# Six edits in one step: a whole-bank gather, S5 powers taken in a pair ahead, one table for small inputs, forget terms in two float32r parts, the last ada chunks inside the routing

## The chip, the cores and the metric

One core of one Trainium2 chip runs the whole program in one launch. The metric is device time in microseconds (us), the median over runs. Everything is float32 in HBM; 580 MB of weights are streamed once through the core's on-chip memory in chunks of [128, 4096] float32 (2 MiB), and the tokens (256 of them, 1024 wide) stay on chip.

## The reference, cut to what matters

Two networks in a row over x [1, 256, 1024]. The first has two blocks, each with a mixer (attention, then pooling) and a mixture of 32 experts, and takes shift, scale and gate from an "ada" product of the condition vector c:

```python
def first_block(x, c, ...):
    c_act = jax.nn.silu(c)
    for i in range(2):
        mod = c_act @ ada_w[i] + ada_b[i]                 # ada_w[i]: [1024, 6*1024]
        sh_m, sc_m, gt_m, sh_f, sc_f, gt_f = jnp.split(mod, 6, axis=-1)
        h = modulate(rmsnorm(x, norm_mix_g[i]), sh_m, sc_m)
        y = fox_attention(h, ...) if i == 0 else pool_mixer(h, ...)
        x = x + gt_m[:, None, :] * y
        h = modulate(rmsnorm(x, norm_ffn_g[i]), sh_f, sc_f)
        y = grouped_moe(h, router_w, router_bias, exp_w1[i], exp_w3[i], exp_w2[i])
        x = x + gt_f[:, None, :] * y
    return rmsnorm(x, norm_final_g)

def fox_attention(h, w_in, f_bias, w_o):                  # 16 heads of 64
    q, k, v, f = jnp.split(h @ w_in, [D, 2 * D, 3 * D], axis=-1)
    F = jnp.cumsum(jax.nn.log_sigmoid(f + f_bias), axis=1)
    logits = q @ k.T * scale + F[t] - F[s]                # the forget terms, causal
    return softmax(logits) @ v @ w_o

def grouped_moe(h, router_w, router_bias, w1, w3, w2):    # best group of 8, then top 2 of 32
    scores = jax.nn.sigmoid(h @ router_w)
    # choose by scores + router_bias; gate = scores of the chosen two, normed
    return sum over the chosen e of gate[e] * ((silu(h @ w1[e]) * (h @ w3[e])) @ w2[e])
```

The second network adds an mLSTM beside an S5 state-space mixer, a feed-forward block, an HGRN2 mixer and another feed-forward block. Of it only the set-up of the S5 coefficients is touched here: the powers of its diagonal and the tap matrices K, which depend on weights alone and are made during the first network's second expert layer.

## The kernel before, in words

**Stages.** Attention with the ada product of both layers (20 to 221 us), routing of layer 0 (to 259), experts of layer 0 (to 698), pooling (to 721), routing of layer 1 (to 766), experts of layer 1 (to about 1247), then the second network (to 1935).

**The weight stream.** Chunks are declared in a fixed order (`need`) and issued as soon as a slot is free (`prefetch`, L204, on SP's DMA queue); `get` hands out a chunk, `free` gives its slot back. There are seven slots (`ringa` 3, `ringb` 4) from the start, and three more (`ringc`) from the end of attention to expert pair 3 of layer 1. SP takes its DMA instructions in order, so a chunk whose slot is not free holds up those behind it. In attention the order is the first four ada chunks, attention weights with ada chunks 4 to 15 between them, the first half of the output weights, ada 16 to 21, the second half of them, ada 22 and 23; then the experts' chunks, six for each pair of experts, 16 pairs a layer.

**Order of the work.** In `attention` and `experts` PE's order is written out by hand (`manual_schedule`). The rest is ordered by a scheduler that simulates the program and takes what it holds to be ready; `tc.issue_after(mark)` keeps an instruction behind a given one. The other engines wait on semaphores.

**Attention.** `att_start` loads x, makes the squares for the norm on DVE (L370) and ACT (L368), and takes ada chunks 0 to 3 on PE (`ada_mm`, L655: the activated c, spread to 32 columns as `crep`, against a chunk; a copy on ACT; then a `turn`, L673, of eight small matmuls that brings the row into columns). Ada chunks 4 to 17 are taken on DVE against `crow`, the row of c spread over all partitions; 18 to 23 on PE again, in three pairs near the end of attention. `forget_gate` makes F, `forget_rows` (L849) spreads F by selection matrices `fsel` into two rows per head, `LA` and `RA`, and `heads` adds the forget terms to the logits with one more matmul of two rows (L869). ACT's DMA queue carries, in this order, the table of vectors `vec`, and small inputs: bif, rw, rb, crow, attn_f, fbias, fsel.

**Routing.** `route` makes the router's products (L948) and the transposed tokens, picks the experts on DVE with many small operations, and counts the tokens per expert (L1006). Beside it `moe` splits the transposed tokens into a high and a low float32r part: two copies on ACT (`full`, `hth`), a subtraction on POOL (L1036, `htl`). `overflow` loads the largest count into a register of every engine and branches on it (L1202, L1203); the branch is not taken here.

**Experts.** Two pairs at a time: `gather` (L1086) multiplies the tokens by a one-hot matrix, for four PSUM banks `pd` of two halves each, four matmuls per half. The eviction of a half is written behind its four matmuls:

```python
for b in range(4):
    pd = pp.tile([128, 2, 256], F32, name="e1", bufs=2)
    for i in range(2):
        ... four matmuls into pd[:, i, :]
        if i: nc.scalar.activation(hg..., pd[:, i, :], ...)      # L1089
        else: nc.vector.tensor_scalar(hg..., pd[:, i, :], ...)   # L1091
```

Then for each pair `up` (L1119, four chunks), `turned` (L1132) and `down` (L1146, two chunks), and `spread_out` (L1170) adds a pair's result. Of the eight gathers of a layer one comes ahead of the loop, and seven in it.

**S5 set-up.** A generator that advances one step per expert pair in layer 1 (pairs 7 to 12). Its tap steps fill one PSUM bank `pk` by pieces (L1449) and add the diagonal on DVE, piece by piece (L1457, `s5K`). Its four power steps each multiply on POOL and DVE (L1383, L1387) into one `stage` and transpose the result on PE (L1474), all in one step.

Of the kernel before, what the change touches and what calls it, by code (L numbers as in the profile page):

```python
# [10 lines left out]
F32 = mybir.dt.float32  # L11
# [33 lines left out]
for _name, _cols in [  # L45
# [3 lines left out]
    ("are", 16), ("aim", 16), ("ldt", 16),  # L49
# [6 lines left out]
def layout(x):  # L56
# [25 lines left out]
    }  # L82
    vec = np.zeros((128, NVEC), np.float32)
# [7 lines left out]
    o["crow"] = g["c"]  # L91
# [3 lines left out]
    sel = np.zeros((17, 2, 4, 128), np.float32)  # L95
    for hd in range(NH):
        q, i = 2 * (hd % 2) + hd // 2 % 2, hd // 4
        sel[hd, 0, i, 32 * q] = 8.0
        sel[16, 0, i, 32 * q + 1] = 1.0
        sel[16, 1, i, 32 * q] = 1.0  # L100
        sel[hd, 1, i, 32 * q + 1] = -8.0
    o["fsel"] = sel
    o["fbias"] = g["attn_f_bias"][0].reshape(NH, 1)
    o["wo"] = kxn(g["attn_w_o"][0], 1024).reshape(128, 2, 4096).transpose(1, 0, 2)
    o["rw"] = g["router_w"].reshape(8, 128, NE).transpose(1, 0, 2)
    o["rb"] = g["router_bias"].reshape(1, NE)
# [32 lines left out]
    bif = np.zeros((36, 1), np.float32)  # L139
    bif[0:4, 0] = g["ab_b_if_2"][0][0:4]  # L140
    bif[32:36, 0] = g["ab_b_if_2"][0][4:8]
    o["bif"] = bif
# [20 lines left out]
class Net:  # L163
# [114 lines left out]
    def consts(self):  # L278
# [345 lines left out]
    def ada_setup(self, P):  # L624
        nc = self.nc
        ca = P.tile([128, KT], F32, name="ca")
        nc.scalar.activation(ca, self.vec("c"), AF.Silu)
        self.crep = P.tile([128, KT, 32], F32, name="crep")
        nc.vector.tensor_copy(self.crep, ca[:, :, None].to_broadcast([128, KT, 32]))
        self.crow = P.tile([128, D], F32, name="crow")  # L630
        nc.scalar.dma_start(self.crow, self.A["crow"].to_broadcast([128, D]))
        nc.scalar.activation(self.crow, self.crow, AF.Silu)
        self.halfsel = P.tile([128, 2], F32, name="halfsel")
# [21 lines left out]
    def ada_mm(self, chunks, wp, pp):  # L655
# [3 lines left out]
        pg = pp.tile([128, 512], F32, name="pL", bufs=2)  # L659
# [7 lines left out]
        row = wp.tile([128, 512], F32, name="adarow", bufs=2)  # L667
        nc.scalar.copy(row, pg)

        def turn():  # L670
            pm = pp.tile([128, n, 4], F32, name="gm")
# [17 lines left out]
    def attention(self):  # L689
        nc, tc = self.nc, self.tc  # L690
        with ExitStack() as es:
# [5 lines left out]
            LA = wp.tile([128, 4, T], F32, name="LA")  # L697
            RA = wp.tile([128, 4, T], F32, name="RA")
# [4 lines left out]
            fb = wp.tile([NH, 1], F32, name="fb")  # L703
            nc.scalar.dma_start(fb, self.A["fbias"])
            fsel = wp.tile([NH + 1, 2, 4, 128], F32, name="fsel")
            nc.scalar.dma_start(fsel, self.A["fsel"])
            with ExitStack() as es1:
                w0 = self.pool(es1, "att0", 1)
                self.maskA = self.mask(wp, self.ramp(w0), OP.is_gt, 8.0 * BIG, nc.gpsimd)
                self.att_start(h, w0, pp)  # L710
# [50 lines left out]
            qk(0, 1, range(4))  # L761
            self.forget_rows(F1, LA, RA, fsel, pp)
# [7 lines left out]
            values(0, 0, range(8))  # L770
            do(1)
            values(0, 1, range(8))
# [1533 lines left out]
```

## Time and profile before

| | us |
|---|---|
| median of three runs | 1944.87 |
| the three runs | 1947.57, 1936.15, 1944.87 |
| profiled execution, its own time | 1936.65 |
| its span in the trace | 1934.9 |
| PE busy in it | 1757.8 (91%) |
| VectorE (DVE) busy | 795.3 (41%) |
| ScalarE (ACT) busy | 541.3 (28%) |
| GpSimd (POOL) busy | 176.5 (9%) |
| mean granted TensorE clock | 0.959 |

The span runs from the first to the last instruction that the profiler shows; the profiled execution's own time has 1.75 us more around it. Busy time of TensorE (PE) is counted apart from its weight loads (PEld), which overlap it. A line such as L1119 is a line of the kernel's code; an arrow `out<-in` names the tiles written and read. In a timeline the brackets hold how long the engine stood idle ahead of the instruction and what released it.

### The profile page before, as it was taken

The page shows a single profiled execution, that of the slowest core. Times are in us where ns is not written, and L with a number is a line of the kernel's source. Part 1 is how long each engine was busy: PE and PEld are TensorE (multiplying, and loading weights), DVE is VectorE, ACT ScalarE, POOL GpSimd, SP SyncE. Part 2 cuts the span into 40 slices and gives each one's busy share as a digit, 9 for nine tenths or more (in the row PEclk, how much of TensorE's full clock was granted, in tenths as well). Part 3 has the DMA queues.
Part 4 walks back from the last instruction along what each step waited for, and adds up shares of the span by engine and source line. Part 5 has one row for each costly group of instructions (what it writes and reads, how often), then busy time and mean ns, then how long its engine had stood idle before and what let it go on. Part 6 is the DMA issues. An engine that isn't in the chain of part 4 may idle for free.

```text
span 1934.9 us, 26697 instructions
## 1 busy us (share of the span) xinstructions
PE 1757.8 (91%) x11274; PEld 1177.5 (61%) x11274; DVE 795.3 (41%) x1532; ACT 541.3 (28%) x958; POOL 176.5 (9%) x263
## 2 busy tenths in 40 slices
PE   4999689999999985999988889899999989999998
PEld 2676434444444454444444333488999989999997
DVE  3676422112111133222542223366655556665554
ACT  2222211111110122101200001154644456555443
POOL 0000100000000001000240333213100002200000
PEclk9899879999999996999989989998999999999999
DMA  9996969999999994999899879822555434344541
GB/s 394 425 349 255 399 262 426 427 427 426 427 427 427 427 426 164 428 426 428 371 400 385 352 306 427 343 71 88 194 195 195 153 137 174 131 192 154 200 169 44
DMA packets 42130, 582.92 MB, mean 301 GB/s; under 512 B 4865, under 2 KB 5249, under 8 KB 6418
## 3 DMA queue, kind: packets, MB, share of 16 engines
q1 hardware_dynamic: 41184, 580.13, 72.9%
q8 instruction: 92, 1.51, 0.3%
q10 hardware_dynamic: 818, 0.98, 0.1%
q14 instruction: 36, 0.29, 0.0%
HBM read 580.05 MB, written 1.05 MB: 300 GB/s over the span
## 4 chain that ended last, share of the span: by engine, by line
PE 52%; DVE 5%; ACT 2%; issue 2%; POOL 1%; DVEq 0%; ACTq 0%; POOLq 0%
PE e L1119 11%; PE py L1898 6%; PE e L1146 6%; PE ph L263 4%; PE ph L264 4%; PE ph L265 4%; PE e L1086 2%; PE q L264 2%; PE q L265 2%; PE q L263 2%; PE yacc L1165 2%; DVE wlo L241 1%; DVE hg L1091 1%; POOL ringb L1387 1%; DVE ringb L1383 1%
## 5 line engine op out<-in xcount | busy, mean ns | idle before, releaser
L241 DVE TENSOR_TENSOR wlo<-ringa,whi 128x1024 fp32r<-128x1024 f32 x190 | 225.9, 1229 | 177.0 <-ACT whi L240 176.9
L240 ACT CAST whi<-ringa 128x1024 fp32r<-128x1024 f32 x192 | 191.5, 1049 | 143.2 <-issue 60.6
L1119 PE MATMUL e<-ringb,hg 128*64 128x512 f32 x1024 | 227.7, 599 | 2.4 <-issue 1.2
L264 PE MATMUL ph<-hlo,whi 128*128 128x256 f32 x704 | 198.0, 281 | 0.6 <-DVE hlo L546 0.6
L263 PE MATMUL ph<-hhi,whi 128*128 128x256 f32 x704 | 198.3, 282 | 0.0
L265 PE MATMUL ph<-hhi,wlo 128*128 128x256 f32 x704 | 197.9, 281 | 0.0
L1126 DVE TENSOR_TENSOR u<-u,e 128x512 f32<-128x512 f32 x32 | 22.0, 688 | 386.2 <-PE e L1119 386.2
L1119 PEld LDWEIGHTS e<-ringb,hg 128*64 128x64 f32 x1024 | 78.8, 139 | 144.2 <-issue 141.2
L264 PEld LDWEIGHTS ph<-hlo,whi 128*128 128x128 f32 x704 | 133.9, 190 | 1.6 <-DVE hlo L546 0.8
L263 PEld LDWEIGHTS ph<-hhi,whi 128*128 128x128 f32 x704 | 134.1, 190 | 0.8
L265 PEld LDWEIGHTS ph<-hhi,wlo 128*128 128x128 f32 x704 | 134.1, 190 | 0.0
L1119 PE MATMUL e<-ringa,hg 128*64 128x512 f32 x592 | 132.9, 598 | 1.0 <-DMA ringa<-in_exp 1.0
L1086 PE MATMUL e<-oh,hth 128*128 128x256 f32 x256 | 80.2, 339 | 55.3 <-DVE hg L1091 43.2
L1146 PE MATMUL e<-ringa,uT 128*64 128x512 f32 x528 | 117.7, 596 | 3.6 <-issue 3.6
L1086 PEld LDWEIGHTS e<-oh,hth 128*128 128x128 f32 x256 | 53.8, 210 | 80.8 <-DVE hg L1091 57.1
L1119 PEld LDWEIGHTS e<-ringa,hg 128*64 128x64 f32 x592 | 45.2, 138 | 83.6 <-issue 83.2
L1119 PE MATMUL e<-ringc,hg 128*64 128x512 f32 x432 | 95.2, 592 | 0.0
L1089 ACT ACTIVATE hg<-e,mod,msc 128x256 f32<-128x256 f32 x64 | 36.2, 565 | 186.7 <-PE e L1086 186.6
L1123 ACT ACTIVATE u<-e 128x512 f32<-128x512 f32 x32 | 19.1, 597 | 233.4 <-PE e L1119 233.4
L1146 PEld LDWEIGHTS e<-ringa,uT 128*64 128x64 f32 x528 | 39.6, 137 | 70.2 <-issue 68.3
L1156 ACT ACTIVATE yh<-e,gs 128x512 fp32r<-128x512 f32 x32 | 22.0, 687 | 202.0 <-PE e L1146 202.0
L1387 POOL TENSOR_TENSOR ringb<-ringb 128x128 f32<-128x128 f32 (+1 forms) x86 | 46.0, 548 | 343.2 <-DVE ringb L1383 220.5
(572 smaller groups left out, 3267.2 us busy)
## 6 DMA issues: line engine op xcount, KB each, us to landing
ringb<-in_exp SPq DMA_DIRECT2D x83, 2048.0 KB, 17.9
ringa<-in_exp SPq DMA_DIRECT2D x70, 2048.0 KB, 15.6
ringc<-in_exp SPq DMA_DIRECT2D x39, 2048.0 KB, 23.4
ringa<-in_f SPq DMA_DIRECT2D x32, 2048.0 KB, 7.4
ringb<-in_ada SPq DMA_DIRECT2D x15, 2048.0 KB, 11.7
ringa<-in_ada SPq DMA_DIRECT2D x9, 2048.0 KB, 16.3
ringa<-in_cin SPq DMA_DIRECT2D x8, 2048.0 KB, 8.2
ringa<-in_attn SPq DMA_DIRECT2D x3, 2048.0 KB, 15.7
```

What stands on the lines that cost most here:

```text
L240: nc.scalar.copy(hi[:, o], raw[:, o])
L241: (eng or nc.vector).tensor_tensor(lo[:, o], raw[:, o], hi[:, o], op=OP.subtract)
L263: mm(ps, wh, ah, start=start, stop=False, **kw)
L264: mm(ps, wh, al, start=False, stop=False, **kw)
L265: mm(ps, wl, ah, start=False, stop=stop, **kw)
L1086: nc.tensor.matmul(pd[:, i, :], htok[h][:, tt, k * 128:(k + 1) * 128], oh[:, tt, :], start=tt + h == 0, stop=tt + h == 2)
L1089: nc.scalar.activation(hg[q][:, k, :], pd[:, i, :], AF.Identity, scale=sc[:, k:k + 1], bias=sh[:, k:k + 1])
L1119: nc.tensor.matmul(ps[s, :], h[:, kt, o:o + 64], w[:, k, ab, :], start=kt == 0, stop=kt == KT - 1)
L1146: nc.tensor.matmul(py[s, :], uT[:, ft, s], w[:, ft, ab, :], start=ft == 0, stop=ft == 3)
L1165: nc.tensor.matmul(yacc[tt][hf], g[:, 128 * tt:128 * tt + 128], y[p][i][:, 512 * hf:512 * hf + 512], start=False, stop=last and i == 1, sk ...
L1387: nc.gpsimd.tensor_tensor(o, a, b, op=op)
L1898: m = nc.tensor.matmul(py[tt][hf], u[x][:, ts_], w[y][:, n], start=ft == 0 and i == 0, stop=ft == NFT - 1 and i == 2)
```

## The change

Six edits are made together.

- **Table.** bif, fbias, the router's bias and weights become columns of `vec` (336 columns before, 626 after), which SP loads ahead of x. ACT's queue is left with two loads, attn_f and fsel. crow is no longer loaded: `spread_row` makes it from the activated c, with eight matmuls and two copies. `crep` goes; the matmul reads the column of c with a broadcast.
- **Forget terms.** F is split into a high and a low float32r part in 48 rows, the selection matrices are float32r with four rows per head, and `LA` and `RA` are float32r. The first values product moves ahead of `forget_rows`.
- **Ada.** Chunks 18 to 23 leave `attention`; `ada_rest` takes them in the routing of layer 0, behind the last transpose of the tokens.
- **Low part of the tokens.** One DVE operation from PSUM in the place of ACT's second copy and POOL's subtraction: two of them are held behind the gate's last operation, two behind `slot`.
- **Gather.** Both evictions of a bank are written behind all eight matmuls.
- **S5.** Taps: the diagonal is added behind all four pieces. Powers: two rooms in place of one stage; the powers of a step are multiplied one or more pairs ahead of the step that transposes them.

```diff
@@ the table VEC
-    ("are", 16), ("aim", 16), ("ldt", 16),
+    ("are", 16), ("aim", 16), ("ldt", 16), ("bif", 1), ("fb", 1), ("rb", NE), ("rw", KT * NE),
...
-    o["crow"] = g["c"]
...
-        nc.scalar.dma_start(self.vt, self.A["vec"])
-        self.bif = P.tile([36, 1], F32, name="bif")
-        if "bif" in self.A:
-            nc.scalar.dma_start(self.bif, self.A["bif"])
+        nc.sync.dma_start(self.vt, self.A["vec"])
+        self.bif = self.vec("bif")
...
     def ada_setup(self, P):
-        ca = P.tile([128, KT], F32, name="ca")
+        ca = self.P1.tile([128, KT], F32, name="ca")
         nc.scalar.activation(ca, self.vec("c"), AF.Silu)
-        self.crep = P.tile([128, KT, 32], F32, name="crep")
-        nc.vector.tensor_copy(self.crep, ca[:, :, None].to_broadcast([128, KT, 32]))
-        self.crow = P.tile([128, D], F32, name="crow")
-        nc.scalar.dma_start(self.crow, self.A["crow"].to_broadcast([128, D]))
-        nc.scalar.activation(self.crow, self.crow, AF.Silu)
...
+    def ada_rest(self, wp, pp):
+        turn = [self.ada_mm(ADA[i:i + 2], wp, pp, ("a0", 1, "m0")) for i in range(18, 24, 2)]
+        for t in turn:
+            t()
...
-                nc.tensor.matmul(pg[q:q + 32, :], self.crep[:, kt, :], w[:, kt, :], start=kt < 4 // n, stop=kt >= KT - 4 // n)
+                nc.tensor.matmul(pg[q:q + 32, :], self.ca[:, kt:kt + 1].to_broadcast([128, 32]), w[:, kt, :], start=kt < 4 // n, stop=kt >= KT - 4 // n)
...
@@ attention
-            LA = wp.tile([128, 4, T], F32, name="LA")
-            RA = wp.tile([128, 4, T], F32, name="RA")
+            LA = wp.tile([128, 4, T], F32R, name="LA")
+            RA = wp.tile([128, 4, T], F32R, name="RA")
...
-            fb = wp.tile([NH, 1], F32, name="fb")
-            nc.scalar.dma_start(fb, self.A["fbias"])
-            fsel = wp.tile([NH + 1, 2, 4, 128], F32, name="fsel")
-            nc.scalar.dma_start(fsel, self.A["fsel"])
+            fb = self.vec("fb")[0:NH, :]
+            fraw = wp.tile([48, 2, 4, 128], F32, name="fraw")
+            nc.scalar.dma_start(fraw, self.A["fsel"])
+            fsel = wp.tile([48, 2, 4, 128], F32R, name="fsel")
+            nc.scalar.copy(fsel, fraw)
...
             qk(0, 1, range(4))
+            values(0, 0, range(8))
             self.forget_rows(F1, LA, RA, fsel, pp)
...
             do(0)
-            values(0, 0, range(8))
+            values(0, 1, range(8))
             do(1)
-            values(0, 1, range(8))
...
             ada(2)
-            t1 = self.ada_mm(ADA[18:20], wp, pp)
+            wo(1, range(0, 4), range(2))
             do(7)
-            t2 = self.ada_mm(ADA[20:22], wp, pp)
+            wo(1, range(4, 8), range(2))
             do(7)
-            t1()
-            wo(1, range(KT), range(2))
-            t2()
             self.route_setup(0, wp, pp, "gm")
             wo(1, range(KT), range(2, 4))
-            self.ada_mm(ADA[22:24], wp, pp)()
...
@@ att_start
+        self.spread_row(crow, self.ca, pp, "pL", 2)
...
@@ forget_gate
+        F1 = wp.tile([48, T], F32R, name="fF1")
+        nc.scalar.activation(F1, self.ones[0:48, 0:1].to_broadcast([48, T]), AF.Copy)
+        nc.scalar.copy(F1[0:NH, :], C)
+        nc.vector.tensor_tensor(F1[32:32 + NH, :], C, F1[0:NH, :], op=OP.subtract)
...
@@ heads
-                b = slice(b, b + 2)
+                b = slice(b, b + 4)
...
@@ moe_setup
-        self.rw = P.tile([128, KT, NE], F32, name="rw")
-        nc.scalar.dma_start(self.rw, self.A["rw"])
-        self.rbias = P.tile([128, NE], F32, name="rbias")
-        nc.scalar.dma_start(self.rbias, self.A["rb"].to_broadcast([128, NE]))
+        self.rw = self.vec("rw").rearrange("p (k n) -> p k n", k=KT)
+        self.rbias = self.vec("rb")
...
@@ route
+        if meanwhile:
+            with tc.issue_after(t.ins):
+                meanwhile(w2, pp)
...
@@ moe
-                gate, slot, mint, r, mark = self.route(wp, w2, pp, xt)
-                with tc.issue_after(mark):
-                    for i in range(4):
-                        o = slice((i % 2) * 512, (i % 2) * 512 + 512)
-                        src, sc = xt[i].rearrange("p a b -> p (a b)"), r[:, i // 2:i // 2 + 1]
-                        full = w2.tile([128, 512], F32, name="full", bufs=2)
-                        nc.scalar.activation(full, src, AF.Copy, scale=sc)
-                        nc.scalar.activation(htok[0][:, i // 2, o], src, AF.Copy, scale=sc)
-                        nc.gpsimd.tensor_tensor(htok[1][:, i // 2, o], full, htok[0][:, i // 2, o], op=OP.subtract)
+                gate, slot, mint, r, marks = self.route(wp, w2, pp, xt, None if l else self.ada_rest)
+                for i, mark in ((0, 1), (2, 1), (1, 2), (3, 2)):
+                    o = slice((i % 2) * 512, (i % 2) * 512 + 512)
+                    src, sc = xt[i].rearrange("p a b -> p (a b)"), r[:, i // 2:i // 2 + 1]
+                    hi, lo = (htok[h][:, i // 2, o] for h in range(2))
+                    with tc.issue_after(marks[0]):
+                        nc.scalar.activation(hi, src, AF.Copy, scale=sc)
+                    with tc.issue_after(marks[mark]):
+                        nc.vector.scalar_tensor_tensor(lo, src, sc, hi, op0=OP.mult, op1=OP.subtract)
...
@@ gather
+                for i in range(2):
+                    k = 2 * b + i
                     if i:
                         nc.scalar.activation(hg[q][:, k, :], pd[:, i, :], AF.Identity, scale=sc[:, k:k + 1], bias=sh[:, k:k + 1])
...
@@ the S5 set-up
+            for jt in range(js, js + 4):
                 nc.vector.scalar_tensor_tensor(s5["K"][:, jt, :], self.ident, self.vec("dskip", jt, 1), pk[:, jt - js, :],
                                                op0=OP.mult, op1=OP.add)
...
+        rooms = [buf[:, o:o + 1024].rearrange("p (i j n) -> p i j n", i=2, j=4) for o in (1024, 2048)]
+        def powers(q):
...
+                o = [rooms[q % 2][:, i, :, 32 * j:32 * j + 32] for i in range(2)]
...
+        def turned(q):
...
+                    nc.tensor.transpose(pt[:, jt, :], rooms[q % 2][:, i, jt, :], self.ident)
+                nc.vector.tensor_copy(s5["B"][:, i, 4 * q:4 * q + 4, :], pt)
+        taps(0)
+        powers(0)
+        yield True
+        taps(4)
+        yield True
+        taps(8)
+        yield True
+        taps(12)
+        powers(1)
+        yield True
+        for q in range(4):
+            turned(q)
+            if q < 2:
+                powers(q + 2)
             yield True
```

`spread_row` is there before too (it makes the gate's row in layer 1): for each of eight columns a matmul of the column, broadcast, with the identity, and a copy for each half of the row.

## Rows read from the trace of the kernel before

**Rows 1.** Windows of the whole span: us, each engine's busy us, granted clock, DMA share, GB/s.

```profile
core 0: us, PE busy (x) PEld busy (x) DVE busy (x) ACT busy (x) POOL busy (x), PEclk, DMA share, GB/s
0.00:43.00 43.00, 17.44 (x168) 9.18 (x168) 9.54 (x53) 11.05 (x19) 2.74 (x11) 1.00 0.96 391
...
95.00:192.00 97.00, 97.00 (x494) 63.84 (x492) 66.82 (x184) 25.31 (x88) 0.62 (x1) 1.00 0.78 302
...
247.00:264.00 17.00, 13.74 (x50) 8.67 (x52) 5.71 (x14) 4.82 (x6) 0.00 (x0) 0.57 0.02 8
264.00:691.00 427.00, 401.64 (x2072) 183.98 (x2070) 80.66 (x144) 45.99 (x74) 0.00 (x0) 1.00 1.00 425
...
766.00:1247.00 481.00, 437.61 (x2476) 199.29 (x2474) 145.79 (x305) 53.92 (x87) 89.25 (x154) 0.97 0.92 386
```

**Rows 2.** Waits of PE, 264 to 700: waited for, us in total, times, longest us.

```profile
PE e L1086 <- DVE hg L1091: 17.9, 28, 0.7
...
PE e L1119 <- DMA ringb<-in_exp: 1.2, 1, 1.2
```

**Rows 3.** Timeline, 0 to 60: start, us, engine, line, operation, out<-in, count [idle before<-releaser].

```profile
10.24 0.75 DVE L370 TENSOR_TENSOR nsq<-x 128x256 f32<-128x256 f32 x2
...
19.96 0.72 ACT L368 ACTIVATE nsq<-x 128x256 f32<-128x256 f32 x2 [10.96 <-DMA rbias<-in_rb]
...
43.42 15.70 PE L607 MATMUL pL<-h,ringa 128*128 128x256 f32 x64 [0.99 <-DVE h L827]
```

**Rows 4.** Timeline of PE, 59 to 130, the forget terms and the first values.

```profile
80.34 6.71 PE L849 MATMUL pL<-fF,fsel 17*128 17x256 f32 x16 [3.65 <-issue]
...
90.74 8.99 PE L732 MATMUL pL<-ringb,h 128*128 128x512 f32 x16
101.77 7.13 PE L732 MATMUL pL<-ringb,h 128*128 128x512 f32 x16
```

**Rows 5.** Groups of PE, 43 to 222: line, operation, count | busy us, mean ns.

```profile
L869 PE MATMUL pQ<-RA,LA 2*128 2x128 f32 (+1 forms) x64 | 10.4, 402 | 0.0
```

**Rows 6.** Timeline of PE, 168 to 265, from the ada chunks to the experts.

```profile
188.51 3.64 PE L664 MATMUL pL<-ringa,crep 128*32 128x512 f32 x32
...
205.17 0.95 PE L673 MATMUL gm<-halfsel,adarow 128*128 128x2 f32 x8
...
215.39 3.64 PE L664 MATMUL pL<-ringb,crep 128*32 128x512 f32 x32
...
220.80 1.07 PE L948 MATMUL m<-x,rws 128*32 128x256 f32 x16
...
236.60 0.41 PE L1006 MATMUL m<-am,ones 128*1 128x32 f32 x4 [10.38 <-DVE am L997]
...
258.79 3.40 PE L1119 MATMUL e<-ringa,hg 128*64 128x512 f32 x8
```

**Rows 7.** Timeline of DVE, 218 to 265, routing of layer 0 and first gather.

```profile
229.56 2.35 DVE L978 SCALAR_TENSOR_TENSOR gq<-gs,gm,revg 128x4 f32<-128x4 f32 x2
...
234.85 0.29 DVE L989 MAX8 v<-selm 128x8 f32<-128x32 f32 x2
...
244.67 0.76 DVE L1071 TENSOR_TENSOR oh<-iota,slot 128x256 fp32r<-128x256 f32 x2 [5.63 <-PEq L1203]
...
256.47 0.76 DVE L1071 TENSOR_TENSOR oh<-iota,slot 128x256 f32<-128x256 f32 x2 [1.31 <-PE e L1086]
```

**Rows 8.** Timeline of POOL, 218 to 265, the first of two subtractions.

```profile
229.40 2.49 POOL L1036 TENSOR_TENSOR htl<-full,hth 128x512 fp32r<-128x512 f32 x2 [6.71 <-ACT hth L1035]
```

**Rows 9.** Timeline, 500 to 562, one gather inside the expert loop.

```profile
518.30 0.38 PE L1086 MATMUL e<-oh,hth 128*128 128x256 f32 x1
...
520.46 0.56 ACT L1089 ACTIVATE hg<-e,mod,msc 128x256 f32<-128x256 f32 x1 [8.32 <-PE e L1086]
...
525.77 0.60 PE L1132 MATMUL e<-ident,u 128*128 128x128 f32 x4
```

**Rows 10.** Waits of PE, 950 to 1165, pairs of layer 1 with S5 work.

```profile
PE e L1474 <- POOL ringb L1387: 10.7, 2, 7.2
...
PE e L1449 <- DVE s5K L1457: 5.9, 12, 0.5
```

More of the change, by code (lines that the diff above doesn't have):

```diff
@@ L82, in layout @@
     }
+    bif, fb = np.zeros((2, 128, 1), np.float32)
+    bif[0:4, 0] = g["ab_b_if_2"][0][0:4]
+    bif[32:36, 0] = g["ab_b_if_2"][0][4:8]
+    fb[0:NH, 0] = g["attn_f_bias"][0]
+    cols.update({
+        "bif": bif, "fb": fb, "rb": np.tile(g["router_bias"], (128, 1)),
+        "rw": g["router_w"].reshape(8, 128, NE).transpose(1, 0, 2).reshape(128, -1),
+    })
     vec = np.zeros((128, NVEC), np.float32)
@@ L94, in layout @@
     o["attn_f"] = w[:, 3072:].reshape(8, 128, NH).transpose(1, 0, 2)
-    sel = np.zeros((17, 2, 4, 128), np.float32)
+    sel = np.zeros((48, 2, 4, 128), np.float32)
     for hd in range(NH):
[L97 to L101, printed above, removed]
+        q, i = 32 * (2 * (hd % 2) + hd // 2 % 2), hd // 4
+        for n in range(2):
+            sel[32 * n + hd, 0, i, q + n] = 8.0
+            sel[32 * n + hd, 1, i, q + 2 + n] = -8.0
+            sel[16, 0, i, q + 2 + n] = 1.0
+            sel[16, 1, i, q + n] = 1.0
     o["fsel"] = sel
-    o["fbias"] = g["attn_f_bias"][0].reshape(NH, 1)
     o["wo"] = kxn(g["attn_w_o"][0], 1024).reshape(128, 2, 4096).transpose(1, 0, 2)
-    o["rw"] = g["router_w"].reshape(8, 128, NE).transpose(1, 0, 2)
-    o["rb"] = g["router_bias"].reshape(1, NE)
     e = np.empty((2, NPAIR, 6, 128, 4096), np.float32)
@@ L709, in attention @@
                 self.maskA = self.mask(wp, self.ramp(w0), OP.is_gt, 8.0 * BIG, nc.gpsimd)
-                self.att_start(h, w0, pp)
+                crow = wp.tile([128, D], F32, name="crow")
+                self.att_start(h, crow, w0, pp)
             wp = self.pool(es, "att1", 1)
@@ L818, in att_start @@
             nc.vector.tensor_tensor(h[:, kt, :], self.x[:, kt, :], r, op=OP.mult)
+        self.crow = crow
+        self.spread_row(crow, self.ca, pp, "pL", 2)
         for j in range(4):
@@ L1002, in route @@
         nc.vector.reciprocal(gsum, gsum)
-        nc.vector.tensor_tensor(gate, gate, gsum.to_broadcast([128, 2, NE]), op=OP.mult)
+        last = nc.vector.tensor_tensor(gate, gate, gsum.to_broadcast([128, 2, NE]), op=OP.mult).ins
         pm = pp.tile([1, NE], F32, name="m0")
@@ L1015, in route @@
         slot = wp.tile([128, 2, NE], F32, name="slot")
-        nc.vector.scalar_tensor_tensor(slot, pr, 1.0, am, op0=OP.add, op1=OP.mult)
-        return gate, slot, mint, r, mark
+        end = nc.vector.scalar_tensor_tensor(slot, pr, 1.0, am, op0=OP.add, op1=OP.mult).ins
+        return gate, slot, mint, r, (mark, last, end)
     def moe(self, l, cap=CAP, between=None):
@@ L1371, in s5_prepare @@
         g = buf[:, 2048:3072].rearrange("p (i j n) -> p i j n", i=2, j=16)
-        stage = buf[:, 2048:3072].rearrange("p (i j n) -> p i j n", i=2, j=4)
         tmp = buf[:, 3072:3584]
@@ L1441, in s5_prepare, with taps @@
             yield True
-        for js in range(0, 16, 4):
+        def taps(js):
             pk = pp.tile([128, 4, 128], F32, name=tag, bufs=bufs)
@@ L1456, in s5_prepare @@
                                          start=i == 0, stop=i == 1, skip_group_check=True)
+            for jt in range(js, js + 4):
                 nc.vector.scalar_tensor_tensor(s5["K"][:, jt, :], self.ident, self.vec("dskip", jt, 1), pk[:, jt - js, :],
                                                op0=OP.mult, op1=OP.add)
[L1459 to L1461 removed]
+        rooms = [buf[:, o:o + 1024].rearrange("p (i j n) -> p i j n", i=2, j=4) for o in (1024, 2048)]
+        def powers(q):
+            b = [v[:, 4 * q:4 * q + 4, :] for v in B]
             for j in range(SL):
[L1463 removed]
+                o = [rooms[q % 2][:, i, :, 32 * j:32 * j + 32] for i in range(2)]
                 if j == SL - 1:
@@ L1480, in s5_prepare @@
         c, n = (cs, sn), 1
-        t1, t2 = (stage[:, i].rearrange("p j n -> p (j n)").rearrange("p (j n) -> p j n", j=16) for i in range(2))
+        t1, t2 = (buf[:, o:o + 512].rearrange("p (j n) -> p j n", j=16) for o in (2048, 2560))
         for k in range(T.bit_length() - 1):
```

34 lines of the change are left out of this document (12 added, 22 removed).

## The prediction

> **What bounds the kernel.** I read the windows first, cutting the span where the stages change [rows 1]. Each stage has another limit. In the first 43 us the DMA engines are 0.96 busy at 391 GB/s and PE does 17.44 us of work: something that lands late sets the start. From 95 to 192 PE is busy without a gap while the stream runs at 302 GB/s, so attention is PE's. From 264 to 691, the experts of layer 0, the stream is the limit: DMA share 1.00 at 425 GB/s, PE 401.64 of 427. The experts of layer 1, 766 to 1247, are PE's again: 386 GB/s, and with PE busy only 437.61 of 481 its own waits. So an edit in layer 0's experts is worth nothing by itself, an edit ahead of them only as much as it moves the stream, and an edit in layer 1's experts its whole PE time until the stream there is full. The second network is not changed.
>
> Then the waits of PE in each stage. In layer 0's experts the evictions of the gather take 17.9 us in 28 waits, and a landing chunk appears only at the end (1.2 us): PE is just barely ahead of the stream [rows 2]. In layer 1 the S5 work adds 10.7 and 5.9 [rows 10].
>
> Sums below are against the profiled execution, 1936.65 us; the median, 1944.87, lies 8.2 above it, within the spread of the runs shown.
>
> **Start.** ACT begins its share of the squares of x at 19.96, after 10.96 us behind a DMA; DVE did the same on x at 10.24 [rows 3]. ACT's queue issues small loads one behind the other; two remain. Gain 19.96 − 10.24 = 9.7, and the chunks allow it: x, the table and the four ada chunks are 9.8 MB, 25 us at 391 GB/s [rows 1], against a first q/k product at 43.42. SP is handed the table (0.3 MB, 0.8 us) ahead of x, the 0.5 MB of crow go; that cancels. spread_row's eight matmuls and two copies lie in the 25 us in which PE has little to do; if that cover were gone they'd cost 2. The new ACT copy of fsel can stand ahead of the squares and wait for fsel's landing: bound of the gain 5 to 10; I take **9.7**, as only two loads are left ahead of it.
>
> **Forget terms.** Values (0,0), moved up, cover the 3.65 us for which PE waits for F; the added copy and subtraction on ACT and DVE (about 1 us) are covered by the same product, some 7 us long. It runs at the full clock there: 8.99 to 7.13, 1.9. The sixteen recorded pieces of L849 (6.71, two to a float32 matmul) halve: 3.3 [rows 4]. L869: 10.4 us for 32 matmuls in two pieces each [rows 5]; a float32r matmul of 256 columns costs at most 0.15 (32 in a gather of 7.47, less four waits of 0.64 [rows 2, 9]), and these are 192 wide on average: 3.7, gain 6.5. Sum **15.4**; if float32r with four rows were no faster here, 5.6.
>
> **Ada chunks out of attention.** Two pairs of 3.64, two turns of 0.95, and 215.39 to 220.80 for the last: **14.6** [rows 6]. The routing then starts 39.7 us earlier, at R = 181.1 where it was 220.80.
>
> **Ada chunks into routing.** Three pairs (3.64 and a copy of some 0.8 before the next, one PSUM buffer) and three turns, 17.8 us, stand on PE behind the transposes, and the count matmul shares a PSUM tag with the turns: it comes at about R+22.5 where it came at R+15.8 [rows 6]. The first up product, 22.2 behind the count before, comes at about R+40, against R+38.0.
>
> What that costs is read from the stream. Six of the seven slots hold ada chunks until the routing; the first expert chunk waits for the slot that the last output weights leave, at R−1. Three go to ringc, six follow as ada pairs are freed at R+9, 13.5 and 18. SP issues them ahead of the branch. At 4.93 us a chunk (2.097 MB at 425 GB/s) ten chunks last until R+48.5; the first up product frees one 5 us after it starts, R+45: the stream does not break. Its last chunk lands at R−1+1+96×4.93 = R+473, 654.5, where it was about 691 [rows 1]: layer 0's experts end **36.5** earlier. The gathers' gain in layer 0, like the faster routing there, vanishes into waits for chunks, about 4 us in each pair.
>
> **Low part on DVE.** Two groups of tiny operations on DVE took 2.35 and 2.42 us [rows 7] exactly while POOL subtracted for 2.49 each [rows 8]; a like pair of operations took 0.29 [rows 7]. Without POOL, 2 × 2.06 = **4.1** in layer 1's routing. The four new DVE operations (about 0.75 each, as the one-hots [rows 7]) go into the wait for the branch, 5.63 us long there. Were these pushed behind the branch: up to 3 lost.
>
> **Gather.** One in the loop takes 518.30 to 525.77, 7.47; four waits of 0.64, and a slow first matmul behind each [rows 2, 9]. With a bank written whole PE goes on to the other bank while two evictions of about 0.56 run. Bounds 2.6 (the waits) to 3.4; I take 3.1, seven times in layer 1: **21.7**. If ACT and DVE read the bank one after the other, 1.1 us against some 1.2 for eight matmuls, the third and fourth bank come about 0.2 late each: 2.7 instead. The Trainium skill ("PSUM — Partial Sum Buffer", section "PSUM bank collisions raise a hardware error") says that two engines may not touch one bank in the same partitions at once, reads included; by that the sum is 3 us smaller, and no row quoted here shows it. The gather ahead of the loop, at a clock of 0.57, takes 11 us (245.4 to 256.4 in layer 0 [rows 1, 7]); its like in layer 1 gains 3.1 × 11/7.47 = 4.6 if all scales with PE's clock; the evictions do not, so I take **3.5**.
>
> **S5.** With the powers made a pair ahead, PE's 10.7 for POOL goes, and the 5.9 for the pieces of the taps: **16.6** [rows 10]. The work is only moved; what is late next is the set-up of the first step on DVE, which stays. Bounds 6 (only the taps) to 20 (restarts too).
>
> Can layer 1's stream carry it? 481 us at 386 GB/s is 185.7 MB; at 425 that is 437, so at most 44 can go, and 21.7 + 16.6 = 38.3 does [rows 1].
>
> **Sum.** 36.5 + 4.1 + 3.5 + 21.7 + 16.6 = 82.4; 1936.65 − 82.4 = **1854**. The terms' bounds: less 10 (start 5, S5 or gathers a few each), more 8.
>
> **Rivals.**
> *A, the stream breaks in the routing.* If the expert chunks stand on SP behind the load of the count, the branch or the first gather, the six slots lie empty: after exp0, landed at R+5, the next is issued at about R+31: 26 lost, 1880. For it: SP takes its instructions in order, and 1.00 share in that stage means nothing is made up later [rows 1]. Against: the order of issue puts them ahead. 0.14.
> *B, attention becomes the stream's.* Attention's 69 MB need 163 us at 425 GB/s, and R−1 is 180: 17 us in reserve, with seven slots and a stream that drops to 302 GB/s in its middle [rows 1]. If it falls 15 behind: 1869. 0.16.
> *C, the orders don't come out as written*: the scheduler leaves the powers and taps where they wait, and evictions serialise: 16.6 + 21.7 × 0.6 lost, 1884. 0.07.
> *D, slower.* In layer 0 PE will wait about 4 us in each pair for a chunk. If its granted clock falls there from 2.4 to 1.2 GHz, a pair's 25.1 us of work (401.64/16) grow to between 37 (by 11.1 to 7.47 for a gather at 0.57 and at 1.00 [rows 1, 7, 9]) and 50, against the stream's 29.6: 8 to 20 lost per pair. Its point: a net loss needs 82/20, over four pairs at the low clock at worst; eight such pairs give 1854 + 160 = 2014. For it: the stretch from 247 to 264, behind the wait for the branch, has 0.57. Against: 264 to 691 shows 1.00 although PE is idle in 25 us of it [rows 1, 2]. The Trainium skill ("TensorE: Matmul & The Clock Gate", section "Why this matters for your kernels") warns that idle gaps between bursts of matmuls bring the half rate back; by it this rival comes true if the waits bunch. 0.04.
> *E, more goes than I count*: the full clock behind shorter gaps, the restarts after each wait, attention's first heads at the full clock: 20 more, 1834. 0.06.
>
> **Chances.** The forecast has 0.53, with its own range 1840 to 1866. The range 1828 to 1885 leaves out D, part of C and the edges, under 2 in 10. About 1% is what a measurement here can tell from no change; faster by more than that holds in all cases but D and an unforeseen wait of 60 us: 0.93, same 0.03, slower 0.04.
>
> **What would show it.** First q/k at about 33; ACT's squares at about 10; no wait ahead of the forget rows; routing at 181; the first up at 221 with the stream's share near 1.00 from 181 to 655; PE's waits for chunks in layer 0 at 50 us and more, and no wait for hg in layer 1; gq and pen under 0.5 us; no wait for POOL ahead of the power transposes. I am wrong if the stream pauses between 181 and 225, if attention shows waits for chunks, or if the clock in layer 0 is under 0.95.

## The result and the profile after

The changed kernel takes 1871.11 us (median of four, 1868.97 to 1871.71) against 1940.51 (1935.08 to 1947.57): ratio 0.9638, 95% interval 0.9600 to 0.9677. The forecast was 1854 with a range of 1828 to 1885: the direction and the range held, and four fifths of the forecast gain came. The profiled execution took 1871.40, its span 1869.6, so it is 65.3 shorter than the profiled one of before, where 82.4 were forecast. By stages, as differences of the moment at which the stage ends (us; the moment is the start of the first or last matmul of its kind, and so it is below where a last down product "ends"):

| stage ends with | before | after | stage's own gain | forecast |
|---|---|---|---|---|
| first q/k product | 43.42 | 33.75 | 9.7 | 9.7 |
| first router product, R | 220.80 | 188.63 | 22.5 | 30.0 |
| last down product, layer 0 | 694.97 | 673.51 | -10.7 | -3.2 |
| first up product, layer 1 | 766.54 | 735.50 | 9.6 | 7.6 |
| last down product, layer 1 | 1246.12 | 1177.95 | 37.1 | 38.3 |
| end of the span | 1934.9 | 1869.6 | -2.9 | 0 |

Of the 82.4, 17.1 are missing. Attention lacks 7.5, layer 0's routing and experts lack 7.5, and the second network gave back 2.9; layer 1's routing gave 2.0 more than forecast and its experts 1.2 less.

The windows of the changed kernel, with the columns of [rows 1]:

```profile
0.00:34.00 34.00, 19.54 (x185) 12.67 (x186) 11.70 (x56) 10.99 (x21) 2.73 (x11) 1.00 0.96 388
...
240.00:250.00 10.00, 9.13 (x48) 3.26 (x44) 0.93 (x2) 1.88 (x2) 0.00 (x0) 1.00 0.65 242
250.00:664.00 414.00, 384.75 (x1986) 171.43 (x1984) 78.38 (x142) 45.41 (x73) 0.00 (x0) 1.00 1.01 427
...
737.00:1190.00 453.00, 429.56 (x2496) 196.24 (x2490) 148.48 (x319) 59.09 (x98) 96.28 (x158) 0.98 0.98 415
```

Layer 0's experts have the stream at its limit as before, with a hole at 240. What is new is the last row: layer 1, at 386 GB/s in [rows 1], now has 415. It has become the stream's as well (the end of the experiments shows how far). The waits of PE say the same, layer 0 (230 to 675) first:

```profile
PE e L1125 <- DMA ringb<-in_exp: 9.8, 9, 1.3
PE e L1125 <- DMA ringc<-in_exp: 6.0, 5, 1.3
PE e L1125 <- DMA ringa<-in_exp: 5.0, 5, 1.3
...
PE e L1090 <- ACT hg L1095: 2.3, 7, 0.4
```

and layer 1 (737 to 1200):

```profile
PE e L1125 <- DMA ringa<-in_exp: 6.6, 1, 6.6
...
PE e L1125 <- DMA ringb<-in_exp: 3.1, 4, 1.2
...
PE e L1090 <- ACT hg L1095: 2.1, 7, 0.3
```

Of the 17.9 us for the gather's evictions [rows 2] 2.3 are left ahead of its matmuls and 2.3 ahead of the transposes behind it; the S5 waits [rows 10] are gone. In their place stand waits for chunks: 20.8 us in layer 0, where the forecast had 50 and more, and 9.7 in layer 1, where it had none. The forecast took some 4 us for every pair of layer 0; but the first wait comes at 469, for until there PE lived on the ten chunks that had landed ahead of it.

### The profile page after: what moved, and what is told of

Its sections match the earlier page's. It is cut to its first block, busy times and chain, and to the rows that moved or that the text cites. A ratio compares the mean times of both kernels' runs of the same rounds, so it can differ in the third digit from the quotient of the medians.

```text
span 1869.6 us, 26564 instructions
## 1 busy us (share of the span) xinstructions
PE 1735.0 (93%) x11250; PEld 1160.7 (62%) x11250; DVE 786.3 (42%) x1541; ACT 535.2 (29%) x951; POOL 168.8 (9%) x255
## 4 chain that ended last, share of the span: by engine, by line
PE 49%; DVE 4%; ACT 3%; DMA 2%; issue 2%; POOL 1%; DVEq 0%; POOLq 0%; ACTq 0%
PE e L1125 11%; PE py L1926 7%; PE e L1152 5%; PE ph L265 4%; PE ph L266 4%; PE ph L264 4%; PE q L265 1%; PE q L266 1%; PE q L264 1%; DMA ringb<-in_exp 1%; PE yacc L1171 1%; DVE wlo L242 1%; DMA ringa<-in_exp 1%; PE e L1090 1%; DVE hg L1097 0%
## 5 line engine op out<-in xcount | busy, mean ns | idle before, releaser
L1125 PE MATMUL e<-ringb,hg 128*64 128x512 f32 x1184 | 262.8, 597 | 13.0 <-DMA ringb<-in_exp 13.0
L1125 PEld LDWEIGHTS e<-ringb,hg 128*64 128x64 f32 x1184 | 89.2, 138 | 178.0 <-issue 161.3
L1392 POOL TENSOR_TENSOR ringa<-ringa 128x128 f32<-128x128 f32 (+1 forms) x86 | 46.5, 553 | 792.1 <-DMA ringb<-in_exp 706.8
L1125 PE MATMUL e<-ringa,hg 128*64 128x512 f32 x432 | 98.2, 604 | 11.6 <-DMA ringa<-in_exp 11.6
L1095 ACT ACTIVATE hg<-e,mod,msc 128x256 f32<-128x256 f32 x64 | 36.2, 565 | 171.0 <-DVE hg L1097 171.0
L1090 PE MATMUL e<-oh,hth 128*128 128x256 f32 x256 | 67.8, 302 | 17.1 <-DVE oh L1075 6.9
L1125 PEld LDWEIGHTS e<-ringa,hg 128*64 128x64 f32 x432 | 34.0, 139 | 73.8 <-issue 69.7
L1159 ACT CAST yh<-u 128x512 fp32r<-128x512 f32 x32 | 19.8, 618 | 196.6 <-DVE u L1158 183.6
## 6 DMA issues: line engine op xcount, KB each, us to landing
ringb<-in_ada SPq DMA_DIRECT2D x15, 2048.0 KB, 16.2
```

The lines of the kernel that those rows point to most:

```text
L1090: nc.tensor.matmul(pd[:, i, :], htok[h][:, tt, k * 128:(k + 1) * 128], oh[:, tt, :], start=tt + h == 0, stop=tt + h == 2)
L1095: nc.scalar.activation(hg[q][:, k, :], pd[:, i, :], AF.Identity, scale=sc[:, k:k + 1], bias=sh[:, k:k + 1])
L1125: nc.tensor.matmul(ps[s, :], h[:, kt, o:o + 64], w[:, k, ab, :], start=kt == 0, stop=kt == KT - 1)
L1392: nc.gpsimd.tensor_tensor(o, a, b, op=op)
```

## Where the time went, line by line

**Start and forget terms.** Timeline of the changed kernel, 0 to 92:

```profile
7.87 0.72 ACT L367 ACTIVATE nsq<-x 128x256 f32<-128x256 f32 x2 [1.63 <-DMA x<-in_x]
...
33.75 15.74 PE L606 MATMUL pL<-h,ringa 128*128 128x256 f32 x64 [1.26 <-DVE h L827]
...
66.89 7.03 PE L734 MATMUL pL<-ringb,h 128*128 128x512 f32 x16
...
75.75 0.71 PE L852 MATMUL pL<-fF,fsel 48*128 48x256 f32 x2 [0.77 <-DVE LA L856]
...
82.18 8.87 PE L734 MATMUL pL<-ringb,h 128*128 128x512 f32 x16
```

ACT squares x as soon as it has landed [rows 3], and the start gains what was forecast, though by other parts: the squares come 12.1 earlier (7.87 for 19.96), but spread_row's matmuls stand on PE's path from 13.86 to 17.51. The first values product runs at full clock, 7.03 for 8.99 [rows 4]; but now the matmuls of the forget rows wait for their evictions, and it is the second product that runs behind them at 8.87, where it had 7.13 (granted clock 0.79 from 82 to 91, 1.00 from 67 to 74). The slow stretch was moved, not removed. And the forget matmuls of the heads:

```profile
L872 PE MATMUL pQ<-RA,LA 4*128 4x256 f32 x16 | 3.3, 403 | 0.0
...
L872 PE MATMUL pQ<-RA,LA 4*128 4x128 f32 x16 | 2.8, 341 | 0.0
```

Busy time fell from 10.4 [rows 5] to 6.1, but busy time of matmuls that overlap counts the same time twice. From the start of these matmuls to the start of the next ones a step took 0.42 and 0.63 before and takes 0.26 and 0.31 now, 0.48 less; the first of the eight steps, at a lower clock both times, gains 0.96. Together that is 4.3.

**Routing and the stream's start.** Timeline, PE, DVE and SP's queue, 188 to 247:

```profile
188.63 0.66 PE L949 MATMUL m<-x,rws 128*32 128x256 f32 x8
...
198.41 0.36 DVE L982 SCALAR_TENSOR_TENSOR gq<-gs,gm,revg 128x4 f32<-128x4 f32 x2
...
210.86 0.28 PE L1010 MATMUL m<-am,ones 128*1 128x32 f32 x4 [0.41 <-DVE mod L676]
...
224.41 0.58 PE L1090 MATMUL e<-oh,htl 128*128 128x256 f32 x1 [4.10 <-issue]
...
232.66 5.24 PE L1125 MATMUL e<-ringb,hg 128*64 128x512 f32 x16
237.73 10.47 PE L1125 MATMUL e<-ringc,hg 128*64 128x512 f32 x48
...
243.02 0.34 SPq L205 DMA_DIRECT2D ringb<-in_exp  x1
```

Without POOL beside it the tiny operation takes 0.36 where it took 2.35 [rows 7, 8]. The count comes at R+22.2, as worked out (22.5). Then two things go otherwise: PE stops for 4.10 us after three matmuls of the gather, with nothing shown that it waits for, and the first up product starts at R+44, not R+40; and the slot it frees at 237.7 is filled only at 243.0. SP's waits from 205 to 260 name the branch:

```profile
SPq L1209 <- SPq L1209: 29.9, 6, 6.3
```

Six waits, the last five about a chunk's 4.93 us apart. In the trace they are semaphore waits that stand in SP's program at the branch's line, one for each of the eight semaphores of its chunks. The last five end within 0.02 us of landings (222.44, 228.06, 232.96, 237.86 and, the tenth chunk's, 242.74), and the eleventh chunk is issued at 243.02. So past the branch SP waits until all chunks in flight have landed, and the stream runs dry. Before, the tenth chunk had landed by 249.5, long ahead of the first freed slot at 263.9, and the same waits (10.8 us of them) cost nothing.

**Gather.** One in the loop, timeline of PE; and, below it, the group of ACT's evictions over the whole span:

```profile
1104.81 0.38 PE L1090 MATMUL e<-oh,hth 128*128 128x256 f32 x1
...
1107.24 0.38 PE L1090 MATMUL e<-oh,hth 128*128 128x256 f32 x1 [0.30 <-ACT hg L1095]
...
1109.69 0.55 PE L1138 MATMUL e<-ident,u 128*128 128x128 f32 x3 [0.28 <-ACT hg L1095]
```

```profile
L1095 ACT ACTIVATE hg<-e,mod,msc 128x256 f32<-128x256 f32 x64 | 36.2, 565 | 171.0 <-DVE hg L1097 171.0
```

4.88 us for 7.47 [rows 9]: 2.6, and 2.5 by the pairs' lengths (28.1 for 30.6). ACT's idle time ends with DVE's eviction, 171.0 us of it: the two evictions of a bank go one after the other, as the Trainium skill ("PSUM — Partial Sum Buffer", section "PSUM bank collisions raise a hardware error") says that they must, and PE waits 0.3 for the second. By that rule the prediction had 2.7.

## The experiments

Theory S was formed from these traces: after the change the stream sets both expert layers, and each edit is worth what it moves the stream. Rival P is the prediction's own sum, term by term. A run's median is given with its range; the changed kernel's is 1871.1. The kernel before, run beside each group of experiments, had medians of 1937.2 to 1939.1, against 1940.5 beside the changed kernel; so differences of 3 us between groups show nothing by themselves, and the traces decide.

**Ada chunks back in attention.** All other edits stay.

```diff
-                gate, slot, mint, r, marks = self.route(wp, w2, pp, xt, None if l else self.ada_rest)
+                gate, slot, mint, r, marks = self.route(wp, w2, pp, xt, None)
...
+            t1 = self.ada_mm(ADA[18:20], wp, pp)
...
+            t2 = self.ada_mm(ADA[20:22], wp, pp)
...
+            self.ada_mm(ADA[22:24], wp, pp)()
```

> The changed kernel with ada chunks 18 to 23 back in attention, as before; all else as changed. Theory S (after the change the stream of chunks sets both expert layers, and ahead of layer 0 only the moment counts at which the eleventh expert chunk can be issued): the routing starts 13 us later, at about 202, but the first ten chunks have landed before the branch and SP issues the eleventh as soon as the first up product frees a slot, at 241 to 244, against 243.0 with the chunks in the routing. Layer 0's end within 3 us of the changed kernel's, time 1867 to 1873. Rival P (the terms of the prediction add up): this edit is worth 14.6 less 4, so undoing it costs about 10: 1881.

1867.43 (1866.21 to 1868.98): 3.7 less than with the edit, not 10 more; as ratios to the kernel before beside each, 0.9643 and 0.9638, the two are the same. The routing starts at 203.66, 15.0 later. Its windows:

```profile
230.00:240.00 10.00, 8.27 (x40) 6.48 (x41) 5.33 (x12) 3.54 (x5) 0.00 (x0) 0.67 0.04 15
240.00:243.00 3.00, 3.00 (x14) 0.88 (x12) 0.81 (x3) 0.00 (x0) 0.00 (x0) 0.79 0.00 0
243.00:246.00 3.00, 3.00 (x16) 0.98 (x14) 0.00 (x0) 0.00 (x0) 0.00 (x0) 1.00 0.60 137
```

The stream stands still for some 12 us with ten chunks landed (the tenth at 232.5; the expectation had them down before the branch, which SP reaches at 217), and starts again at 243.3 with the first freed slot, 0.3 us from where the changed kernel's does. Layer 0's last down product ends at 674.00 (673.51 there). So the 15 us of PE time bought nothing. The 3.7 come later, most of them in the second network, whose code is the same: its stretch from layer 1's last down product to the end was 687.6 to 691.7 in these kernels; differences below 4 us are not explained here.

**Gather as before.** Evictions behind each half's four matmuls.

```diff
-                for i in range(2):
-                    k = 2 * b + i
                     if i:
```

> The changed kernel with the eviction of each half behind its own four matmuls, as before. Theory S: layer 0's end does not move (the stream sets it); in layer 1 PE needs 7 times 2.5 us more in the loop and about 4 in the gather ahead of it, but the 9.7 us that PE now waits for chunks take up their share: plus 11 to 13, 1882 to 1885. Rival P: the whole term comes back, 21.7 and 3.5: 1896.

1881.06 (1879.51 to 1883.96): plus 10.0, just under S's 11 to 13, where P had 25. Layer 1's waits for chunks are gone, its pairs with a gather are back at 30.6, and from first up to last down product it is 4.9 longer, where S had 7.8.

**S5 as before.**

> The changed kernel with the S5 taps and powers in the order of before. Theory S: pairs 7 to 13 of layer 1 get 29 us longer on PE (as the two traces' pairs show), of which the 9.7 us of waits for chunks take up their share: plus 19 to 20, 1890 to 1892. Rival P: 16.6, 1888, with the waits for chunks still there. Rival without any limit by the stream: plus 29, 1900.

1890.14 (1889.58 to 1894.04): plus 19.0. The waits for POOL (10.7) and for the diagonal (5.9) are back, with 8.1 for a chunk besides. S has the time, but not for its reason: it wanted the 9.7 us of waits for chunks to be taken up, and 8.1 us of such waits stand, as P said. By the trace layer 1 is 23.0 longer, and the stages ahead of it 2.9 shorter, which this edit doesn't explain. The rival without any limit (plus 29) is out; S and P lie too near for this run alone.

**Forget terms as before.**

> The changed kernel with the forget terms of before: one float32 part in 17 rows, LA and RA float32 with two rows per head, the first values product behind the first heads. Theory S: the routing starts 9.4 us later (waits 3.7, the selection matmuls 1.3, the values 0.2, and 0.5 for each of eight heads' steps), and as the expert stream starts from there, the time grows by as much: 1880 to 1881. Rival P: the full 15.4, 1886. Rival of a stream that swallows it: under 3.

1880.80 (1875.29 to 1883.29): plus 9.7, near S's 9.4 and under P's 15.4 in every execution. The profiled one is the fastest, 3.9 more than the changed kernel's: in it attention is 7.0 longer and the start 1.2, the first expert chunk is issued 8.3 us later, the eleventh 7.1 (250.14, behind the landing of the tenth at 249.9, though the first up product starts at 236.33), and layer 0's last down product ends 7.1 later.

**One and two pairs in the routing**, the others in attention; the second is

```diff
-        turn = [self.ada_mm(ADA[i:i + 2], wp, pp, ("a0", 1, "m0")) for i in range(18, 24, 2)]
+        turn = [self.ada_mm(ADA[i:i + 2], wp, pp, ("a0", 1, "m0")) for i in range(20, 24, 2)]
...
             ada(2)
+            t1 = self.ada_mm(ADA[18:20], wp, pp)
...
+            t1()
```

> The changed kernel with one of the three ada pairs (chunks 22, 23) in the routing and two in attention. Theory S: layer 0's end is set by the eleventh expert chunk's issue. One pair hides behind DVE's choice of experts, so the first up product stands at about 233 and frees a slot at 238.5, the first ten chunks have landed by then and SP issues at once; layer 0's last down product ends at about 669, 4 to 5 us before the changed kernel's 673.5. Time 1863 to 1869 (the second network's order can shift by 3 us from kernel to kernel). Rival P (terms add up): the two pairs back in attention cost 9: 1880.

> The changed kernel with two of the three ada pairs (chunks 20 to 23) in the routing, one in attention. Theory S: the first up product at about 231 frees a slot at 236.5; the tenth chunk lands at about 236 (first one issued at about 184), so SP, which leaves the branch only when the chunks in flight have landed, issues the eleventh at 236 to 238; the last down product ends at about 667, time 1861 to 1868. Rival P: one pair back in attention costs 4.5: 1875.

1863.36 (1863.23 to 1867.12) and 1862.93 (1860.29 to 1864.43). P is out by 12 and more. With two pairs S is right in its steps: first up product at 230.55, eleventh chunk at 235.28 (0.28 behind the landing of the tenth), last down product at 665.83, 7.7 earlier than in the changed kernel. With one pair S hit the time by luck: the first up product stood at 237.64, not 233, for the same 4.3 us stop of PE and a later count, and layer 0 ended at 673.65, no earlier; its 7.7 (4.3 between the two profiled spans) lie behind layer 0 and are not explained.

**S5 alone, and S5 with the gather, on the kernel before.**

> The kernel before with the S5 part of the change alone (taps with the diagonal behind all four pieces, powers a pair ahead in two rooms). Theory S: the stream in layer 1 has 44 us of slack there, so all 29 us of PE time count: 1937 less 29 is 1908. Rival P: the two waits alone, 16.6: 1920.

> The kernel before with the S5 part and the whole-bank gather, nothing else. Theory S: PE is spared 29 and 17.5 and about 4.5 ahead of the loop in layer 1, but the stream lets layer 1 become only about 37 shorter from first up to last down; with 4.5 ahead of each layer's loop that is 46: 1891. Rival without the stream's limit: 56, 1881. Rival P: 16.6, 21.7, 3.5: 42, 1895.

1912.70 (1909.21 to 1916.22), 24.5 less than the 1937.2 beside it, between S and P; by the trace layer 1 is 27.0 shorter (452.6 for 479.6 from first up to last down product), so P's 16.6 is too little. With the gather as well: 1890.15 (1887.59 to 1891.48), 47 less, as S had it, where 56 were to be had without the stream's limit. Of the 9 that lack, 5.7 are waits for chunks; 3.1 are a stop of PE ahead of the taps, about as long with S5 alone, which goes with S5's 27 in place of 29. What S5 gave beyond its two waits is in part a pair that held neither of them (they stand at 1094 and 1136),

```profile
954.00:992.00 38.00, 33.14 (x142) 17.61 (x140) 25.90 (x48) 6.01 (x9) 34.49 (x31) 0.82 0.94 392
...
970.00:980.00 10.00, 6.58 (x26) 5.70 (x27) 3.08 (x6) 1.70 (x3) 9.38 (x9) 0.59 1.00 426
```

in the kernel before (the pair that starts at 954, and ten us of it), and in the one with S5 alone:

```profile
951.60:982.60 31.00, 28.19 (x142) 13.59 (x140) 19.88 (x52) 6.00 (x9) 26.75 (x30) 1.00 1.01 428
```

The same 142 matmuls have 33.14 us at a granted clock of 0.82 and 28.19 at 1.00. In the kernel before PE waits there 2.95 us, until 971.5, for an eviction of the gather on DVE, which is busy with small S5 operations ahead of it; behind that wait PE works on at a granted clock of 0.50 from 972 to 984. With S5 alone DVE is through with these operations sooner, and no wait of the pair is over 0.6. The edit doesn't touch them; why they come sooner is not shown.

**No branch.**

```diff
-            self.overflow(l, htok, gate, slot, mint, cap)
```

> The changed kernel without the load of the largest count and the branch on it, in both layers; it leaves out the path for an expert with more tokens than it has room for. Theory S: SP no longer waits for the chunks in flight, so it issues the eleventh chunk when the first up product has freed a slot; the stream's pause of about 5 us at 240 goes, layer 0's last down product ends 5 to 6 us earlier, at about 668, and layer 1, set by its stream from the first freed slot on, starts 5.5 us earlier: 1858 to 1862. The stop of PE of 4.1 us in the first gather of layer 0 goes with the branch if it belongs to it. Rival (the pause is one of slots alone, since six hold ada chunks until the routing): the pause stays at 3 us or more, and only layer 1's 5.5 are won: 1866.

1861.77 (1858.43 to 1867.49). Its windows over the place of the hole:

```profile
235.00:240.00 5.00, 3.74 (x22) 1.66 (x20) 1.79 (x3) 0.00 (x0) 0.00 (x0) 1.00 1.00 426
240.00:245.00 5.00, 5.00 (x26) 2.04 (x24) 2.20 (x5) 0.69 (x1) 0.00 (x0) 1.00 1.01 429
```

and SP's waits from 205 to 260, all for PE to free a slot:

```profile
SPq L205 <- PE e L1124: 36.3, 7, 18.2
```

The stream runs through, layer 0's last down product ends 4.0 earlier (669.52; S had 5 to 6), and PE's stop of 4.1 is gone. Part of this comes from PE, which is 9.3 us earlier here (first up product 223.39); but the slot of 237.7 in the changed kernel was free and stayed empty until SP's last wait, which slots don't explain.

**A faster version:** two pairs, and the first gates, the gate's row and the turn behind the first up product.

```diff
         gather(0)
-        gates(0)
-        if l:
-            self.gb = wp.tile([128, D], F32, name="gb")
-            self.spread_row(self.gb, self.gatec(l, 1), pp, "e1", 2)
-            self.turn(yacc)
         for p in range(NPAIR):
             more = p // 2 + 1 < NPAIR // 2
             u = up(p)
+            if not p:
+                gates(0)
+                if l:
+                    self.gb = wp.tile([128, D], F32, name="gb")
+                    self.spread_row(self.gb, self.gatec(l, 1), pp, "e1", 2)
+                    self.turn(yacc)
```

> The changed kernel with two ada pairs in the routing, as in k2, and in each expert layer the first gates, in layer 1 also the gate's row and the turn of x into the accumulators, behind the first up product where they stood ahead of it. Theory S: layer 1's stream starts when the first up product frees a slot, and so 6.9 us earlier (gates, row and turn took 728.6 to 735.5); PE has waits for chunks of that size to give up: 1863 less 5 to 7, 1856 to 1858. In layer 0 nothing, as SP waits for the chunks in flight. Rival (PE is the limit in layer 1): no change, 1863.

1856.36 (1855.67 to 1860.19), ratio to the kernel before 0.9577 (0.9562 to 0.9591), 6.6 under the version with two pairs and 14.7 under the changed kernel. Timeline of PE:

```profile
719.51 10.52 PE L1126 MATMUL e<-ringb,hg 128*64 128x512 f32 x48
729.87 3.60 PE L1126 MATMUL e<-ringa,hg 128*64 128x512 f32 x16
733.40 0.66 PE L1107 MATMUL e<-ident,oh 128*128 128x128 f32 x4
```

The first up product of layer 1 comes 8.8 us earlier than in the version with two pairs (728.33), the stream restarts as much earlier, and the last down product ends 5.6 earlier; layer 0's stays (666.00). PE's work is the same, only its order is other. That alone doesn't decide for the stream, since the new order also spares PE itself some 4 us of waits for DVE and of slower matmuls ahead of the first down product.

**The stream's part, over all these runs.** From the issue of the eleventh chunk to the end of layer 0's last down product it is 430.5 to 430.7 us in the changed kernel and in the seven versions of it that keep the branch (243.02 to 673.51, with two pairs 235.28 to 665.83), whatever PE's part is. That is S for layer 0. In layer 1, from the first chunk that is issued behind a freed slot to the landing of the last, it is 430.4 to 431.4 us in the changed kernel and in five versions (ada chunks or forget terms as before, one and two pairs, no branch), and 431.6 with S5 and the gather on the kernel before: there the stream is full. It is 434.6 in the fastest version, 436.2 with the gather as before and 445.5 with S5 as before, so there PE has its part in layer 1; in the kernel before it is 465.7.

## Why the prediction held, and where its sum was off

- **Start, 9.7:** the size came by luck, from other parts: the squares 12.1 earlier, spread_row 3.7 on the path (it was counted as covered, and with 2 if not), 1.7 back at the first ada chunk (1.92 for 3.64, not explained), and 0.6 lost around the last one, which lands at 28.71. The cause, ACT's wait for small loads, is right.
- **Forget terms, 15.4, measured 9.5 by the two traces and 7.0 when taken back:** the wait of 3.65 went. The selection matmuls gained 1.3 for 3.3, since their evictions hold them (80.34 to 86.98 before, 73.85 to 79.18 after); the two values products 0.2 for 1.9, as the slow clock passed from one to the other; the heads 4.3 for 6.5, since busy time was taken for time on the path.
- **Ada chunks, 14.6 in attention less 3 behind:** the PE time went (13 of it, a wait of 1.3 for DVE came in). The step that failed is "the stream does not break", and beneath it the account: without the move the ten chunks land 11 us ahead of the first freed slot (232.5 and 243.3) and the stream waits for it, with the move the tenth lands at 242.7 and the stream goes on at the same moment. Taken back, it cost nothing. This is rival A's place with another cause and a smaller price: SP had issued the ten chunks in time, but left the branch late. The pause is 4.0 of the 7.5 that layer 0 lacks; most of the rest lies in the ten chunks themselves, which had landed at R+54.1 where the prediction had R+48.5.
- **Low part on DVE, 4.1:** right (2 × 2.0). **Gather ahead of the loop, 3.5:** 4.8 by the traces (745.34 to 757.81, now 720.93 to 728.61). The first up product of layer 0 came at R+44.0; the 40 isn't what its two figures give (22.5 and 22.2 are 44.7), yet without PE's stop of 4.1 it would have been met.
- **Gather, 21.7:** 17.5 to 18.2, seven times 2.5 or 2.6: the lower bound of the range given, a little under what one eviction behind the other was to give.
- **S5, 16.6:** 27 with S5 alone, above the upper bound of 20. The two waits were read rightly; the term lacks what else the order of S5's work did, the wait of 2.95 and the low clock behind it in a pair that holds neither.
- **"44 can go, and 38.3 does":** the two errors above met the stream. PE was spared about 46, and 9.7 came back as waits for chunks, so the stage's sum, 37.1, was nearly right by luck.
- **Small slips of the sums:** the ada work in the routing adds up to 16.2 by the terms named, not 17.8, and 10.4 less 3.7 is 6.7, not 6.5; neither moves the forecast by as much as 2.
- **Rival B** did not come: no wait for a chunk in attention. **Rival D** neither: clock 1.00 in layer 0 with 19 waits of up to 1.3 us; the Trainium skill's warning of idle gaps ("TensorE: Matmul & The Clock Gate", section "Why this matters for your kernels") is borne out by the pair at 954 in the kernel before, where the clock is 0.50 from 972 to 984 behind a wait of 2.95, and not by gaps of up to 1.3.

Open: what holds PE for 4 to 5 us in the first gather, and up to 4 us in the second network between kernels.

## What to carry to other kernels

Work that is moved out of a stage ahead of a stream gains only if the stream starts sooner by it: look for the moment at which the first slot is freed and at what the queue's issuer waits for then. An order that brings the first consumer of the stream forward (two pairs, the first up product ahead of the gates) was worth 14.7 us here; 15 us of PE time ahead of it were worth nothing. Gains in a stage that one resource bounds are to be summed against the next resource's floor, and time on the path is read from start to start, not from busy time.

## What the runs showed that was not expected

PE stops after two to four matmuls of layer 0's first gather: 4.10 us in the changed kernel, 5.2 with the ada chunks in attention, 4.4 with the gather and 4.5 with S5 as before, 4.3 and 4.1 with one and two pairs, 3.9 in the fastest. There is none without the branch, none in layer 1, where the DMA share is 0.07, and none in the kernel before. Load on the DMA engines alone does not make it: with the forget terms as before the branch stands and the share is 0.99 to 1.02 from 220 to 235, and PE doesn't stop. One more trace speaks to it. The DMA records have transfers of instructions besides the chunks, of 16 KB on queue 8, in the expert layers one for about every 256 matmuls and weight loads of PE. In each of the seven kernels that stop, such a transfer ends 1.3 to 1.5 us before PE goes on (at 222.96 and 224.41 in the changed one). So PE may well wait there for its next instructions; no wait in the profile names them, and no run moved them, so this stays unproven.

And SP, once past an untaken branch, issued nothing before the chunks in flight were down: 243.02 in the changed kernel, for a slot that was free at 237.7.
